# Strassen-like forms made in the attention's output projection, and three more pairs by seven products

## Chip, cores and metric

One core of one Trainium2 chip runs the whole program in one launch. The metric is device time in microseconds (us) of one execution; the result is the median of several. The profile is one execution taken by the hardware profiler. TensorE is called PE, VectorE DVE, ScalarE ACT, GpSimd POOL and SyncE SP, as in the profile.

## The reference

A two-layer trunk on x (512 tokens, width 1024) with a memory of 256 tokens, all in float32. Layer 0 has a hybrid attention mixer, layer 1 an mLSTM mixer; both then have memory cross-attention and a gated convolutional feed-forward network. Cut to what matters:

```python
def conv_ffn(xn, w_up, conv_w, conv_b, w_down):
    h = causal_depthwise_conv(xn @ w_up, conv_w) + conv_b
    g, u = jnp.split(h, 2, axis=-1)
    return (jax.nn.gelu(g) * u) @ w_down

for layer in range(2):
    ...
    x = x + mixed
    x = x + memory_cross_attention(rms_norm(x, xattn_norm[layer]), rms_norm(mem, mem_norm[layer]), ...)
    x = x + conv_ffn(rms_norm(x, ffn_norm[layer]), ffn_w_up[layer], ffn_conv_w[layer],
                     ffn_conv_b[layer], ffn_w_down[layer])
return rms_norm(x, final_norm)
```

The up-projection has 2 x 2816 columns, so 44 blocks of 128. Block p of the gate half and block p of the other half make pair p, with p from 0 to 21. Each pair gives 128 rows of activations for the down-projection.

## The kernel before

Everything is kept transposed: x is eight tiles `x[k]` of 128 features by 512 tokens. A float32 product is made of three matmuls: each operand is split into a high part in the matmul's format and a low remainder (`split`: a copy on ACT, then `sub` on DVE), and `mm3` (L274 to L276) adds high x high, high x low and low x high in PSUM.

**Cross-attention** (`xattn`). `Plan` orders tasks by a time model of PE, ACT and DVE and by priority. Its last stage is `p_out`, the output projection: for each of eight blocks m, 24 matmuls of 512 columns, then `xadd` (L495, x += block) and `xprep` (L469 to L476: the scaled split of x for the next stage, and the sum of squares for its norm).

**Feed-forward** (`ffn_steps`). `Sched` lists tasks for PE, ACT, DVE, SP and POOL, each with a duration, dependencies, a due time as priority, and slots of buffers, and emits them in the order of a simulated run; the framework then orders each engine's instructions from that. `clock` is the sum of PE's durations so far, so `at` is PE's planned time at a pair's start.

- A *plain* pair is two blocks of 8 x `mm3` at 512 columns: 48 matmuls. DVE subtracts the two weights' low parts (1024 columns each) and takes two blocks out of PSUM (L1299).
- A pair by *seven products* treats weights and x as 2 x 2 blocks (the halves of the pair, the halves of the features, the halves of the tokens). Seven products of 12 matmuls at 256 columns replace eight, 84 matmuls in all. Four of them (`p6`, `p5`, `p7`, `p4`) take sums of x's blocks as the moving operand: these *forms* T1 to T4 are made once a layer, in four tiles `th[k]`, `tl[k]` of high and low parts. The weights' sums are made anew for each pair: SP loads half of both blocks into `sa`, POOL's accumulating DMA adds the other block onto it (L1318), DVE makes two more sums (L1340, L1346), and five splits follow. Between products DVE combines blocks (L1380, 256 columns each, through scratch tiles `v`, `u2`, `u3`), and L1401 scales the pair.
- `tail` does the convolution (ACT L1256, four DVE taps L1263), the gelu, the product and the split of the activations `ah`, `al`. For pairs 20 and 21 its due times are 25 us earlier.
- `fill` puts *down* blocks between the products: the down-projection goes by chunks of 4, 4, 4, 4 and 6 pairs, eight blocks each; a block of the first four chunks is 12 matmuls of 512 columns on a weight loaded to `dr`. Chunk c's eight blocks are queued once its pairs are done, at pair 5, 9, 13 and 18; a plain pair takes two, a seven-product pair three. At pair 19 the rest of the queue is cut, and its last four blocks are kept for after pair 21 (`late`). Then the last chunk follows, in layer 1 in `finish`.

Before, `SEVEN` holds pairs 4 to 15 and 17 to 20, 16 of 22. The forms are made by `forms` (L1229 to L1242) during pairs 0 and 1, through the rows `hs` and `sa` as scratch. DVE starts a layer's feed-forward with the last `xprep`, then these forms and the norm's root between pair 0's weights.

Of the kernel before, what the change touches and what calls it, by code (L numbers as in the profile page):

```python
# [9 lines left out]
F32 = mybir.dt.float32  # L10
# [15 lines left out]
SEVEN = (4, 5, 6, 7, 8, 9, 10, 11, 12, 13, 14, 15, 17, 18, 19, 20)  # L26
# [106 lines left out]
class Task:  # L133
    def __init__(self, eng, dur, fn, deps, prio, take, free, lat):
        self.eng, self.dur, self.fn, self.prio, self.lat = eng, dur, fn, prio, lat
        self.deps = [d for d in deps if d is not None]
        self.take, self.free = take, free
        self.end = None


class Sched:
# [8 lines left out]
    def add(self, eng, dur, fn, deps, prio, take=(), free=(), lat=0.25):  # L150
        t = Task(eng, dur, fn, deps, prio, take, free, lat)
        t.n = len(self.tasks)
        self.tasks.append(t)
        return t
# [8 lines left out]
    def run(self):  # L163
# [56 lines left out]
class Builder:  # L220
# [154 lines left out]
    def p_out(self, pl, src, mixed, kdeps, gain, gi, order, prio, reload=False, order0=None):  # L375

        state = {}
        done = []
        for m in range(KB8):
            e = self.p_proj(  # L380
                pl, src[m], mixed, lambda ps, m=m: self.xadd(m, ps, reload), (("D", 0.6),), kdeps=kdeps, order=order, prio=prio + m
            )
            done.append(
                pl.add(lambda m=m: self.xprep(m, gain, gi, state), 0, [e], prio + m, chain=(("A", 0.52), ("D", 0.66), ("A", 0.52)), order=[order0])
            )
        self.state = state
        self.xdone = {k: [d] for k, d in enumerate(done)}
# [337 lines left out]
    def mix0(self):  # L725
        nc, t, tc = self.nc, self.t, self.tc
        with tc.tile_pool(name="mix0", bufs=1, reuse_waits="tile") as mp:
# [61 lines left out]
            def gates(ps):  # L789
                z = rows["z"] = self.til(self.memp, "mem", bufs=8)[:8, :]  # L790
# [135 lines left out]
    def p_memory(self, pl, layer, at, step, order=()):  # L926
# [16 lines left out]
        for k in range(KB8):  # L943

            def prep(k=k):
                both = self.til(mp, "mem", (P, 2, MEM), F32R, bufs=8)
# [46 lines left out]
    def xattn(self, layer):  # L993
        nc, t, tc = self.nc, self.t, self.tc
        with tc.tile_pool(name=f"xa{layer}", bufs=1, reuse_waits="tile") as mp:
            self.mp = mp
            pl = Plan(self.plan, [st["banks"][0] for st in self.fills], s=2, w=2, e=4, q=2, pt=2, wt=3)
            self.pad(mp, 192)
            kth = mp.tile([P, KB8, MEM], F32R, name=f"kth{layer}")
            ktl = mp.tile([P, KB8, MEM], F32R, name=f"ktl{layer}")  # L1000
            self.pad(mp, 64)
            vh = mp.tile([P, 2, DM], F32R, name=f"xvh{layer}")
            vl = mp.tile([P, 2, DM], F32R, name=f"xvl{layer}")
# [4 lines left out]
            for h in range(4):  # L1008
# [49 lines left out]
                def ptget(pts=pts):  # L1058
# [36 lines left out]
                for d in range(2):  # L1095

                    def weigh(h=h, d=d, pts=pts):
# [5 lines left out]
                        mh[b], ml[b] = (self.til(mp, "mixed", dtype=F32R, bufs=8) if h < 2 else self.til(self.memp, "mem", dtype=F32R, bufs=8) for _ in range(2))  # L1103
# [5 lines left out]
            self.p_out(pl, t["xo"][layer], lambda: (mh, ml), kd, "ffn", layer, None, 100)  # L1109
# [8 lines left out]
    def ffn_steps(self, layer, mp):  # L1118
# [23 lines left out]

        def raw_tile(st, tag):
            pool, n, bufs = RAWS[tag]
            st[tag] = self.til(pool, tag, (P, n), bufs=bufs)
            return st[tag]

        def load(st, tag, src, cols, at):
# [4 lines left out]
            return add("SP", 0.0017 * cols, fn, (), at, [(tag, st)], (), 4.0)  # L1153
# [60 lines left out]

        self.pad(mp, 192)
        th, tl = ([mp.tile([P, 1024], F32R, name=f"t{i}{layer}{k}", tag=f"t{i}{k}") for k in range(4)] for i in "hl")
        formed, pads = [], []
# [3 lines left out]

        def forms(k, at):

            st = {}

            def scaled(j):
                if j == 0:
                    st["t"] = hs2[st["_hs"]][:, :, 2:514]
                nc.scalar.activation(st["t"][:, j, :512], self.x[k + 4 * j][:], AF.Identity, scale=self.col("ffn", layer * 8 + k + 4 * j))  # L1229

            def first():
                st["r"] = raw_tile(st, "sa")[:]
                tt_(out=pair(st["r"][:, :512]), in0=pair(st["t"][:, 0, :512]), in1=st["t"][:, :, 256:512], op=ALU.subtract)

            T1, T3, T2, T4 = (slice(256 * i, 256 * i + 256) for i in range(4))
            tt_ = nc.vector.tensor_tensor
            a = add("ACT", ACV, lambda: scaled(0), (), at, [("hs", st)])
            a = add("ACT", ACV, lambda: scaled(1), [a], at)
            a = add("DVE", tt(512), first, [a], at, [("sa", st)])
            a = add("DVE", tt(256), lambda: tt_(out=st["r"][:, T2], in0=st["t"][:, 1, 256:512], in1=st["r"][:, T1], op=ALU.add), [a], at)  # L1240
            a = add("DVE", tt(256), lambda: tt_(out=st["r"][:, T4], in0=st["t"][:, 1, 0:256], in1=st["r"][:, T2], op=ALU.subtract), [a], at, (), [("hs", st)])
            h = add("ACT", act(1024), lambda: nc.scalar.copy(th[k][:], st["r"]), [a], at)  # L1242
            formed.append(add("DVE", tt(1024), lambda: self.sub(tl[k][:], st["r"], th[k][:]), [h], at, (), [("sa", st)]))


        def tail(p, st, deps, at):
# [28 lines left out]
            def hi():  # L1275
                acts[p] = tuple(self.til(mp, n, dtype=F32R, bufs=10) for n in ("ah", "al"))
# [32 lines left out]
        def seven(p, fill):  # L1309
# [11 lines left out]
            b1 = load(sa, "sa", up2[p][:, :, :512], 1024, at - 20.0)  # L1321
# [4 lines left out]
            def small(s, tag):  # L1326
                if tag == "s4" and not pads:
                    pads.append(self.pad(mp, 64))
                s["wh"], s["wl"] = (self.til(mp, tag + i, (P, 512), F32R, bufs=1) for i in "hl")
# [39 lines left out]
            p6 = pe(n, lambda: opened("Y", by, "acc", s2, 0, *T2, "Y", True), [w2, *formed], [("acc", by)], [("s2", s2)])  # L1369
# [13 lines left out]
            tmp = lambda n_: (lambda: st[n_][:])  # L1383
# [27 lines left out]
        def down(c, m, steps=1):  # L1411
# [8 lines left out]
            e = add("DVE", 0.6, lambda: self.xadd(m, d["ps"]), [last, xadded[m], *formed], clock[0] + 3.0, (), [("w", d)])  # L1420
# [218 lines left out]
    def finish(self, mp, ah, al):  # L1639
# [7 lines left out]
        outs = [self.til(mp, f"t{i}{k}", (P, 1024), F32R, bufs=1).bitcast(F32)[:, s] for k in range(4) for i in "hl" for s in (slice(0, 512),)]  # L1647
# [20 lines left out]
        def write(ps, t, f, r, vector):  # L1668
            out = outs.pop(0)
            if vector:  # L1670
                nc.vector.tensor_scalar(out=out[:], in0=ps[:], scalar1=r, scalar2=None, op0=ALU.mult)
            else:
                nc.scalar.activation(out[:], ps[:], AF.Identity, scale=r)
            (nc.sync if f else nc.scalar).dma_start(self.t["y"][t][:, f * 512 : f * 512 + 512], out[:])
# [33 lines left out]
    def run(self):  # L1708
        tc = self.tc
        M = bass.MemoryType.PSUM  # L1710
        with (
# [10 lines left out]
            for layer in range(2):  # L1722
                with tc.tile_pool(name=f"mem{layer}", bufs=1, reuse_waits="tile") as self.memp:
                    (self.mix0, self.mix1)[layer]()
                    self.xattn(layer)
                self.ffn(layer)
# [88 lines left out]
```

## Time and profile before

| what | us |
|---|---|
| median of 3 runs | 1497.57 (1497.55 to 1497.65) |
| profiled execution | 1497.39 |
| its span, first to last instruction | 1495.6 |
| PE busy in the span | 1483.6 |
| DVE busy | 1194.5 |
| ACT busy | 806.0 |
| POOL busy | 57.8 |
| feed-forward of layer 0, on PE | from about 416.7 to 765 |
| feed-forward of layer 1, on PE | from about 1139.6 to 1484 |

The page's first part gives busy time by engine, its second the span in 40 slices of 37.4 us with the busy share in tenths. The stage windows give each engine's busy time between two moments; a number in brackets counts instructions that touch the window. In the instruction rows the first number is the start, the second the duration, then engine, line, operation and tiles. In grouped rows "busy, mean ns" and the idle time before follow the bar.

### The profile page before, as it was taken

How to read it: one execution, taken by the hardware profiler on the slowest of the kernel's cores; microseconds unless marked ns; L12 is line 12 of the kernel's file. 1: busy time of each engine (PE TensorE's matmuls, PEld its weight loads, DVE VectorE, ACT ScalarE, POOL GpSimd, SP SyncE). 2: the span in 40 equal slices, each digit the busy share in tenths (PEclk: the TensorE clock that was granted, in tenths of full speed). 3: DMA queues.
4: the chain of work that ended last, by engine and by line, in shares of the span. 5: the costliest groups of instructions: out<-in, count | busy, mean ns of one | idle time of the engine just before them, and what ended most of it. 6: DMA issues, size and time to landing. Idle time of an engine off the chain costs nothing.

```text
span 1495.6 us, 22361 instructions
## 1 busy us (share of the span) xinstructions
PE 1483.6 (99%) x8426; PEld 1281.9 (86%) x8426; DVE 1194.5 (80%) x2255; ACT 806.0 (54%) x1349; POOL 57.8 (4%) x100
## 2 busy tenths in 40 slices
PE   9999999999999999999999999999999999999998
PEld 7888777888889999999888778888888899998987
DVE  7779795666589999989768857666567999999974
ACT  7777573444466455555446634444444655555544
POOL 0000130000001000000000000000000000000000
PEclk9999999999999999999999999999999999999999
DMA  5212223323237665542232222323323756564322
GB/s 195 85 63 79 85 86 115 125 74 125 85 127 192 168 157 154 148 120 89 75 99 85 71 99 84 99 93 120 113 72 126 183 156 169 149 162 134 94 65 76
DMA packets 60796, 171.76 MB, mean 115 GB/s; under 512 B 6672, under 2 KB 6672, under 8 KB 60688
## 3 DMA queue, kind: packets, MB, share of 16 engines
q1 hardware_dynamic: 55072, 152.43, 31.2%
q0 software_dynamic: 4608, 16.78, 6.6%
q8 instruction: 66, 1.08, 0.3%
q10 hardware_dynamic: 1008, 1.12, 0.2%
q14 instruction: 42, 0.34, 0.1%
HBM read 168.21 MB, written 2.10 MB: 114 GB/s over the span
## 4 chain that ended last, share of the span: by engine, by line
PE 93%; DVE 4%; ACT 2%; issue 1%; DMA 0%; SPq 0%; DVEq 0%; ACTq 0%
PE acc L274 19%; PE acc L276 19%; PE acc L275 19%; PE w L275 5%; PE w L274 5%; PE w L276 5%; PE s L274 3%; PE acc L335 2%; PE s L276 2%; PE acc L337 2%; PE acc L336 2%; PE s L275 2%; PE w L1603 1%; DVE wl L265 1%; PE s L401 1%
## 5 line engine op out<-in xcount | busy, mean ns | idle before, releaser
L274 PE MATMUL acc<-xh,wh 128*128 128x512 f32 (+1 forms) x832 | 301.3, 362 | 0.0
L276 PE MATMUL acc<-xh,wl 128*128 128x512 f32 (+1 forms) x832 | 296.8, 357 | 0.0
L275 PE MATMUL acc<-xl,wh 128*128 128x512 f32 (+1 forms) x832 | 296.6, 356 | 0.0
L265 DVE TENSOR_TENSOR wl<-raw,wh 128x1024 fp32r<-128x1024 f32 (+2 forms) x201 | 240.5, 1197 | 44.2 <-ACT wh L268 39.9
L268 ACT CAST wh<-raw 128x1024 fp32r<-128x1024 f32 (+2 forms) x137 | 140.6, 1029 | 164.7 <-PE acc L275 97.5
L275 PEld LDWEIGHTS acc<-xl,wh 128*128 128x128 f32 x832 | 157.2, 189 | 22.0
L276 PEld LDWEIGHTS acc<-xh,wl 128*128 128x128 f32 x832 | 156.2, 188 | 22.7
L274 PEld LDWEIGHTS acc<-xh,wh 128*128 128x128 f32 x832 | 156.3, 188 | 22.1
L1263 DVE SCALAR_TENSOR_TENSOR c<-hs,vec,c 128x512 f32<-128x512 f32 x176 | 128.8, 746 | 4.5 <-ACT c L1256 3.7
L275 PE MATMUL w<-al,wh 128*128 128x512 f32 x304 | 118.6, 390 | 0.0
L274 PE MATMUL w<-ah,wh 128*128 128x512 f32 x304 | 118.5, 390 | 0.0
L276 PE MATMUL w<-ah,wl 128*128 128x512 f32 x304 | 118.4, 389 | 0.0
L1256 ACT ACTIVATE c<-hs,vec 128x512 f32<-128x512 f32 x88 | 69.8, 813 | 52.9 <-DVE hs L1401 46.5
L276 PEld LDWEIGHTS w<-ah,wl 128*128 128x128 f32 x304 | 57.0, 188 | 12.0
L274 PEld LDWEIGHTS w<-ah,wh 128*128 128x128 f32 x304 | 57.1, 188 | 10.2
L275 PEld LDWEIGHTS w<-al,wh 128*128 128x128 f32 x304 | 57.1, 188 | 10.1
L495 DVE TENSOR_TENSOR x<-w,x 128x512 f32<-128x512 f32 x72 | 49.3, 685 | 16.1 <-PE w L276 16.1
L274 PE MATMUL acc<-mem,wh 128*128 128x256 f32 (+1 forms) x192 | 61.5, 320 | 0.0
L276 PE MATMUL acc<-mem,wl 128*128 128x256 f32 (+1 forms) x192 | 61.0, 318 | 0.0
L275 PE MATMUL acc<-mem,wh 128*128 128x256 f32 (+1 forms) x192 | 60.8, 317 | 0.0
L495 DVE TENSOR_TENSOR x<-acc,x 128x512 f32<-128x512 f32 x32 | 22.1, 690 | 46.6 <-PE acc L276 46.6
L1165 ACT CAST wh<-dr 128x512 fp32r<-128x512 f32 x64 | 39.5, 617 | 35.7 <-PE w L275 18.4
(373 smaller groups left out, 3798.2 us busy)
## 6 DMA issues: line engine op xcount, KB each, us to landing
raw<-in_up_dram SPq DMA_DIRECT2D x56, 512.0 KB, 3.3
dr<-in_down_dram SPq DMA_DIRECT2D x64, 256.0 KB, 2.9
sa<-in_up_dram SPq DMA_DIRECT2D x32, 512.0 KB, 3.5
sa<-in_up_dram POOLq DMA_DIRECT2D x32, 512.0 KB, 5.6
raw<-in_xk_dram SPq DMA_DIRECT2D x16, 512.0 KB, 3.2
raw<-in_wo_dram SPq DMA_DIRECT2D x16, 512.0 KB, 3.3
raw<-in_xq_dram SPq DMA_DIRECT2D x16, 512.0 KB, 3.2
raw<-in_xv_dram SPq DMA_DIRECT2D x16, 512.0 KB, 3.2
```

What stands on the lines that cost most here:

```text
L265: self.nc.vector.tensor_tensor(out=lo, in0=v, in1=hi.bitcast(F32), op=ALU.subtract)
L268: self.nc.scalar.copy(hi, v)
L274: mm(out, wh, xh, start=first, stop=False, skip_group_check=parts)
L275: mm(out, wh, xl, start=False, stop=False, skip_group_check=parts)
L276: mm(out, wl, xh, start=False, stop=last, skip_group_check=parts)
L335: mm(ps, xh[k][:, ts], wh[:, ws], start=(k == 0), stop=False)
L336: mm(ps, xh[k][:, ts], wl[:, ws], start=False, stop=False)
L337: mm(ps, xl[k][:, ts], wh[:, ws], start=False, stop=(k == 7))
L495: self.nc.vector.tensor_tensor(out=self.x[m][:], in0=ps[:], in1=self.x[m][:], op=ALU.add)
L1165: nc.scalar.copy(st["wh"][:, :cols], st[tag][:, :cols])
L1256: nc.scalar.activation(st["c_"][:, j, :], hs()[:, j, 2:514], AF.Identity, scale=self.col("cw", (layer * 3 + 2) * 44 + blk), bias=self.col( ...
L1263: nc.vector.scalar_tensor_tensor(out=c, in0=hs()[:, j, n : n + 512], scalar=w, in1=c, op0=ALU.mult, op1=ALU.add)
```

## The change

Pairs 3, 16 and 21 go by seven products too, so pairs 3 to 21 without a gap. `forms` is taken out of the feed-forward. `p_forms`, a task of the attention's plan, makes the same forms with the same operations; `p_out` of the cross-attention visits its blocks in the order 0, 4, 1, 5, 2, 6, 3, 7, so that form k follows as soon as x[k] and x[k + 4] are done. Two empty planner tasks stand for this work at the start of the feed-forward's plan. A task can have an earliest time (`after`), and the loads of the weight sums of pairs 3, 4 and 5 have one, 16 us ahead of the pair. The late list keeps six blocks in place of four; five are in the queue by then.

To hold the forms from one stage to the next, tiles move: a pool `kv` of four tiles holds the attention's keys and values and then the forms; the memory's tiles stay open as `mem0` to `mem7` and serve, in turn, the memory, half of the attention's outputs, and in the feed-forward `s2`, `a22`, `ra`, `dr` and one `sb`; `v` lies in the memory's norm tile, `u2` and `u3` in the scratch `sqt` of two buffers. `finish` writes its output through the `kv` tiles.

```diff
-SEVEN = (4, 5, 6, 7, 8, 9, 10, 11, 12, 13, 14, 15, 17, 18, 19, 20)
+SEVEN = (3, 4, 5, 6, 7, 8, 9, 10, 11, 12, 13, 14, 15, 16, 17, 18, 19, 20, 21)
...
-                    at = 0.0 if e == "-" else now[e]
+                    at = t.after if e == "-" else max(now[e], t.after)
...
-    def p_out(self, pl, src, mixed, kdeps, gain, gi, order, prio, reload=False, order0=None):
+    def p_out(self, pl, src, mixed, kdeps, gain, gi, order, prio, reload=False, order0=None, ms=range(KB8), after=None):
...
+            if after and m >= 4:
+                after(m - 4, done[m] + done[m - 4], prio + n)
...
+    def p_forms(self, pl, layer, k, deps, prio):
...
+        th, tl = self.form(0, k), self.form(1, k)
+        def one():
+            g = st["g"] = self.til(self.mp, "pth", (P, 2, 512), F32)
+            r = st["r"] = self.til(self.mp, "ptl", (P, 2, 512), F32)[:].rearrange("p a b -> p (a b)")
+            for j in range(2):
+                nc.scalar.activation(g[:, j, :], self.x[k + 4 * j][:], AF.Identity, scale=self.col("ffn", layer * 8 + k + 4 * j))
+            tt(out=r[:, :512].rearrange("p (a b) -> p a b", a=2), in0=g[:, 0, :].rearrange("p (a b) -> p a b", a=2), in1=g[:, :, 256:512], op=ALU.subtract)
+            tt(out=r[:, T2], in0=g[:, 1, 256:512], in1=r[:, T1], op=ALU.add)
+            tt(out=r[:, T4], in0=g[:, 1, 0:256], in1=r[:, T2], op=ALU.subtract)
+        def two():
+            nc.scalar.copy(th, st["r"])
+            self.sub(tl, st["r"], th)
+        a = pl.add(one, 0, deps, prio, chain=(("A", 1.04), ("D", 1.28)))
+        pl.add(two, 0, [a], prio, chain=(("A", 0.95), ("D", 1.14)))
...
-            self.p_out(pl, t["xo"][layer], lambda: (mh, ml), kd, "ffn", layer, None, 100)
+            self.p_out(pl, t["xo"][layer], lambda: (mh, ml), kd, "ffn", layer, None, 100, ms=(0, 4, 1, 5, 2, 6, 3, 7), after=lambda *a: self.p_forms(pl, layer, *a))
...
+        HOMES = {}
+        for n, (tag, i) in enumerate([("s2h", 0), ("s2l", 0), ("a22h", 0), ("a22l", 0), ("ra", 0), ("dr", 0), ("dr", 1), ("sb", 1)]):
+            HOMES[tag, i] = f"mem{n}"
...
+        add("DVE", 4.0, None, (), -20.0)
+        add("ACT", 3.0, None, (), -20.0)
...
-            b1 = load(sa, "sa", up2[p][:, :, :512], 1024, at - 20.0)
+            b1 = load(sa, "sa", up2[p][:, :, :512], 1024, at - 20.0, at - 16 if p < 6 else 0.0)
...
-            p6 = pe(n, lambda: opened("Y", by, "acc", s2, 0, *T2, "Y", True), [w2, *formed], [("acc", by)], [("s2", s2)])
+            p6 = pe(n, lambda: opened("Y", by, "acc", s2, 0, *T2, "Y", True), [w2], [("acc", by)], [("s2", s2)])
...
-                st["v_"] = self.til(mp, "v", (P, 256), bufs=1)
+                st["v_"] = self.til(self.memp, f"memrb", (P, 256), bufs=1)
...
-                    st[tag] = self.til(mp, tag, (P, 256), bufs=1)
+                    st[tag] = self.til(self.sp, "sqt")[:, :256]
...
-                queue, late = queue[:-4], queue[-4:]
+                queue, late = queue[:-6], queue[-6:]
             (seven if p in SEVEN else plain)(p, fill if p >= 5 else lambda: None)
-            if p < 2:
-                for k in (2 * p, 2 * p + 1):
-                    forms(k, clock[0] + 4.0 * (k % 2))
...
-                self.ffn(layer)
+                    with tc.tile_pool(name=f"kv{layer}", bufs=1, reuse_waits="tile") as self.kvp:
+                        self.pad(self.kvp, 192)
+                        self.kv = [self.til(self.kvp, f"kv{i}", (P, 2048), F32R, bufs=1) for i in range(4)]
+                        self.xattn(layer)
+                        self.ffn(layer)
```

More of the change, by code (lines that the diff above doesn't have):

```diff
@@ L133, with __init__ @@
 class Task:
-    def __init__(self, eng, dur, fn, deps, prio, take, free, lat):
-        self.eng, self.dur, self.fn, self.prio, self.lat = eng, dur, fn, prio, lat
+    def __init__(self, eng, dur, fn, deps, prio, take, free, lat, after):
+        self.eng, self.dur, self.fn, self.prio, self.lat, self.after = eng, dur, fn, prio, lat, after
         self.deps = [d for d in deps if d is not None]
@@ L148, in __init__, with add @@
         self.turn = {r: 0 for r in res}
-    def add(self, eng, dur, fn, deps, prio, take=(), free=(), lat=0.25):
-        t = Task(eng, dur, fn, deps, prio, take, free, lat)
+    def add(self, eng, dur, fn, deps, prio, take=(), free=(), lat=0.25, after=0.0):
+        t = Task(eng, dur, fn, deps, prio, take, free, lat, after)
         t.n = len(self.tasks)
@@ L373, in xs @@
         return self.xh, self.xl
-    def p_out(self, pl, src, mixed, kdeps, gain, gi, order, prio, reload=False, order0=None):
+    def p_out(self, pl, src, mixed, kdeps, gain, gi, order, prio, reload=False, order0=None, ms=range(KB8), after=None):
         state = {}
-        done = []
-        for m in range(KB8):
+        done = {}
+        for n, m in enumerate(ms):
             e = self.p_proj(
-                pl, src[m], mixed, lambda ps, m=m: self.xadd(m, ps, reload), (("D", 0.6),), kdeps=kdeps, order=order, prio=prio + m
+                pl, src[m], mixed, lambda ps, m=m: self.xadd(m, ps, reload), (("D", 0.6),), kdeps=kdeps, order=order, prio=prio + n
@@ L382, in p_out @@
             )
-            done.append(
-                pl.add(lambda m=m: self.xprep(m, gain, gi, state), 0, [e], prio + m, chain=(("A", 0.52), ("D", 0.66), ("A", 0.52)), order=[order0])
-            )
+            done[m] = [pl.add(lambda m=m: self.xprep(m, gain, gi, state), 0, [e], prio + n, chain=(("A", 0.52), ("D", 0.66), ("A", 0.52)), order=[order0])]
+            if after and m >= 4:
+                after(m - 4, done[m] + done[m - 4], prio + n)
         self.state = state
-        self.xdone = {k: [d] for k, d in enumerate(done)}
+        self.xdone = done
@@ new lines, in p_forms @@
+    def p_forms(self, pl, layer, k, deps, prio):
+        nc = self.nc
+        tt = nc.vector.tensor_tensor
+        T1, T3, T2, T4 = (slice(256 * i, 256 * i + 256) for i in range(4))
+        th, tl = self.form(0, k), self.form(1, k)
+        st = {}
+        def one():
[11 more added lines that the diff above has]
+        pl.add(two, 0, [a], prio, chain=(("A", 0.95), ("D", 1.14)))
@@ L389, in evac_tok, with form @@
+    def form(self, i, k):
+        return self.kv[2 * i + k // 2][:, k % 2 * 1024 : k % 2 * 1024 + 1024]
     def evac_tok(self, ps, r, hi, lo):
@@ L1102, in weigh @@
                         b = 2 * h + d
-                        mh[b], ml[b] = (self.til(mp, "mixed", dtype=F32R, bufs=8) if h < 2 else self.til(self.memp, "mem", dtype=F32R, bufs=8) for _ in range(2))
+                        if b == 0:
+                            self.pad(mp, 64)
+                        mh[b], ml[b] = (
+                            self.til(mp, "mixed", dtype=F32R, bufs=8) if h < 2 else self.til(self.memp, f"mem{2 * b - 8 + i}", dtype=F32R, bufs=1) for i in range(2)
+                        )
                         self.split(mh[b][:], ml[b][:], ps[:])
@@ L1212, in norm @@
             return add("ACT", 0.52, None, [c], c.prio)
+        th, tl = ([self.form(i, k) for k in range(4)] for i in range(2))
+        pads = []
         self.pad(mp, 192)
-        th, tl = ([mp.tile([P, 1024], F32R, name=f"t{i}{layer}{k}", tag=f"t{i}{k}") for k in range(4)] for i in "hl")
-        formed, pads = [], []
         hs2 = [mp.tile([P, 2, 514], F32, name=f"hs{layer}{i}") for i in range(2)]
@@ L1220, in ffn_steps @@
             nc.gpsimd.memset(h[:, :, 0:2], 0.0)
[L1222 to L1243, printed above, removed]
+        add("DVE", 4.0, None, (), -20.0)
+        add("ACT", 3.0, None, (), -20.0)
         def tail(p, st, deps, at):
@@ L1419, in down @@
                     joined([last], last.prio, [("act", acted[first + k].st)])
-            e = add("DVE", 0.6, lambda: self.xadd(m, d["ps"]), [last, xadded[m], *formed], clock[0] + 3.0, (), [("w", d)])
+            e = add("DVE", 0.6, lambda: self.xadd(m, d["ps"]), [last, xadded[m]], clock[0] + 3.0, (), [("w", d)])
             xadded[m] = e
@@ L1646, in finish @@
         HALF = [slice(0, 256), slice(256, 512)]
-        outs = [self.til(mp, f"t{i}{k}", (P, 1024), F32R, bufs=1).bitcast(F32)[:, s] for k in range(4) for i in "hl" for s in (slice(0, 512),)]
+        outs = [kv[:, 512 * i : 512 * i + 512] for kv in (self.til(self.kvp, f"kv{i}", (P, 2048), bufs=1) for i in range(2)) for i in range(4)]
         def add(m, ps, c):
```

38 lines of the change are left out of this document (22 added, 16 removed).

## The prediction

> **What bounds the kernel now.** I read the page first, then TensorE's waits, then stages of the feed-forward network (the stage windows), and last VectorE's instructions in order of time.
>
> ```profile
> span 1495.6 us, 22361 instructions
> PE 1483.6 (99%) x8426; PEld 1281.9 (86%) x8426; DVE 1194.5 (80%) x2255; ACT 806.0 (54%) x1349; POOL 57.8 (4%) x100
> DVE  7779795666589999989768857666567999999974
> ...
> PE s L436 <- DVE sqt L430: 1.8, 5, 0.7
> PE acc L514 <- DVE ones L506: 1.1, 1, 1.1
> ```
>
> TensorE (PE) is busy for 99% of the span, and its longest sum of waits on one cause is 1.8 us. So time falls only where matmul time falls, and only as long as the others keep up. The row of VectorE (DVE) names the one that may not: most of its nines lie in the two feed-forward stages, where the change acts. The profiled execution took 1497.39 us, 1.8 more than its span; the median is 1497.57, and I carry differences over to it.
>
> ```profile
> core 0: us, PE busy (x) PEld busy (x) DVE busy (x) ACT busy (x) POOL busy (x), PEclk, DMA share, GB/s
> 645.42:656.30 10.88, 10.88 (x49) 9.01 (x48) 9.84 (x14) 5.62 (x8) 0.00 (x0) 1.00 0.29 97
> 584.20:596.73 12.53, 12.53 (x110) 12.53 (x108) 11.99 (x20) 7.60 (x12) 0.86 (x1) 1.00 0.64 166
> 496.73:499.46 2.73, 2.73 (x14) 2.25 (x13) 2.73 (x6) 1.24 (x2) 0.00 (x0) 1.00 0.69 134
> 606.38:609.55 3.17, 3.08 (x25) 2.87 (x24) 3.13 (x6) 1.67 (x2) 0.00 (x0) 1.00 0.67 226
> 1329.15:1332.17 3.02, 3.02 (x25) 2.85 (x24) 3.02 (x6) 1.67 (x2) 0.00 (x0) 1.00 0.61 197
> 405.80:416.68 10.88, 10.88 (x50) 9.01 (x49) 6.36 (x8) 4.40 (x6) 0.00 (x0) 1.00 0.34 104
> 428.85:461.98 33.13, 33.13 (x147) 27.40 (x146) 31.04 (x45) 23.26 (x31) 1.86 (x2) 1.00 0.51 144
> 477.38:512.00 34.62, 34.62 (x230) 31.68 (x229) 34.51 (x56) 19.83 (x31) 0.86 (x2) 1.00 0.56 146
> 645.42:717.78 72.36, 72.32 (x481) 66.24 (x480) 65.47 (x99) 37.49 (x57) 0.87 (x1) 1.00 0.31 87
> ```
>
> The first row is plain pair 16 of layer 0: 48 matmuls of 512 columns (a count takes in the neighbour at the edge). The second holds nine products of 12 matmuls of 256 columns (108 weight loads). The third is one down block. In the eighth DVE works 34.51 of 34.62 us, and PE still loses nothing: DVE can be full without holding PE.
>
> **Term 1: the products.** A plain pair costs PE 10.88 us. A pair by seven products costs 7 x 12.53 / 9 = 9.75. That is 1.13 less a pair. Pairs 3, 16 and 21 change in both layers: 6 x 1.13 = 6.80 us off PE. The granted clock is 1.00 in all these rows, so no clock enters.
>
> The Trainium skill ("TensorE: Matmul & The Clock Gate", section "Back-to-back issue gap") gives an isolated spacing of N/2.4 + 2.5 ns, 109 ns at 256 columns and 216 at 512; by it, as an estimate, the six pairs would give 6 x (48 x 0.2158 - 84 x 0.1092) = 7.1 us. The rows show 116 and 227 ns, so the measured 6.80 is used.
>
> **Term 2: the forms.** A form is, on ACT, two scalings of 512 and a copy of 1024; on DVE three small sums and a subtraction over 1024. How long DVE takes from one start to the next, when it is full, stands here:
>
> ```profile
> 464.84 0.68 DVE L1340 TENSOR_TENSOR sb<-sa,raw 128x512 f32<-128x512 f32 x1
> 465.45 0.68 DVE L265 TENSOR_TENSOR s4l<-sb,s4h 128x512 fp32r<-128x512 f32 x1
> 466.05 1.22 DVE L265 TENSOR_TENSOR wl<-raw,wh 128x1024 fp32r<-128x1024 f32 x1
> 467.18 0.42 DVE L1380 TENSOR_TENSOR u<-acc,v 128x256 f32<-128x256 f32 x1
> 467.52 0.74 DVE L1263 SCALAR_TENSOR_TENSOR c<-hs,vec,c 128x512 f32<-128x512 f32 x1
> 468.18 0.69 DVE L265 TENSOR_TENSOR s2l<-sb,s2h 128x512 fp32r<-128x512 f32 x1
> ```
>
> By these starts a subtraction or sum over 512 takes 0.605 us, over 1024 1.13, over 256 0.34, a convolution tap 0.66. A form is then 0.605 + 2 x 0.34 + 1.13 = 2.42 us of DVE, four a layer 9.7. ACT's part comes from these two groups: 2 x 0.71 + 1.04 = 2.5.
>
> ```profile
> L1229 ACT ACTIVATE hs<-x,vec 128x512 f32<-128x512 f32 x8 | 5.5, 713 | 0.0
> L1242 ACT CAST th<-sa 128x1024 fp32r<-128x1024 f32 x4 | 4.2, 1042 | 1.9 <-DVE sa L1241 1.9
> ...
> 419.74 0.68 DVE L470 TENSOR_TENSOR sq<-sq,sqt 128x512 f32<-128x512 f32 x1
> 420.34 0.69 DVE L1233 TENSOR_TENSOR sa<-hs 128x512 f32<-128x512 f32 x1
> ```
>
> In their new place two output blocks take PE 10.88 us (window 405.80:416.68) beside 6.36 of DVE and 4.40 of ACT. One form more makes 8.8 and 6.9, still below 10.88: cost 0. Without that cover it would be up to 2.4 us a form. Only the fourth has no output block after it. But in before the first form already starts at 420.34, right behind the last square sum at 419.74, so the fourth takes a place that was taken, and the norm's chain behind it is no later: 0, bounded by one form, 2.4 us, if PE stood for it. The forms issue no DMA. The new order of the blocks changes no count.
>
> The feed-forward start loses 9.7 us of DVE work and gains a seven-product pair. Such a pair takes DVE 7 x 0.605 + 3 x 1.13 + 5 x 0.34 + 4 x 0.66 = 11.97 us; a plain pair takes 4 x 0.605 + 2 x 1.13 + 4 x 0.66 = 7.32. The difference is 4.65, so about 5 us of DVE come free while PE loses 1.13. In window 428.85:461.98 DVE had 31.04 of 33.13. I expect no stall from DVE there.
>
> **Term 3: pairs 16 to 21, where DVE gets tight.** No down blocks are queued in pairs 16 and 17, three in pair 18; the longer late list takes the one of pair 19. In before, window 645.42:717.78 has DVE at 65.47 of 72.36. The change adds 4.65 for pair 16, and for pair 21 the part before its products end: 11.97 less its tail and the last two steps (0.34 + 1.13 + 4 x 0.66 + 2 x 0.605 = 5.3) against 2.87 for the plain one (two weight subtractions, one evacuation): 3.8. It takes away one down block's 2 x 0.605 = 1.2. DVE: 72.7 us. PE: 72.36 - 2 x 1.13 - 2.73 = 67.4. By that DVE is 5.3 us short. This is the upper bound, since the busy time counts instructions that stood alone at their full duration, 0.08 above the spacing of a full DVE; were all 99 such, 7.9 us would be recovered and nothing be short. So the shortage lies in -2.6 to 5.3 us a layer.
>
> What covers it: the five late blocks, 5 x 2.73 = 13.65 us of PE for 6 us of DVE. They need no result of pairs 16 to 21, so the planner can pull one forward where a product waits. Then only the end counts: pair 21's activation must be ready for the last chunk.
>
> ```profile
> 725.72 0.69 DVE L265 TENSOR_TENSOR al<-c,ah 128x512 fp32r<-128x512 f32 x1
> ```
>
> In before it ends at 726.41, 8.63 after PE left the pairs at 717.78, and four late blocks (10.9) cover it. After: 8.63 + 0.34 + 1.22 - 0.69 = 9.5, plus a backlog of up to 5.3: 14.8 at most. Five blocks give 13.65, and the last activation is read only by the sixth step of the next block, 5 x 0.68 = 3.4 later: 17.05. Covered; if blocks are pulled forward, both sides shrink alike.
>
> What remains is small: a product that finds its operand late. Before shows the size behind pairs without down blocks: 24 small matmuls took 3.17 and 3.02 (windows 606.38 and 1329.15), where 24 x 12.53 / 108 = 2.78 is normal: 0.39 and 0.24. After has four such places more a layer (pairs 3, 16, 19, 21). I take 0.25 each, 1.0 a layer, 2.0 in all, near these rows; the bounds are -0.3 a layer (the present losses vanish too) and 5.3.
>
> **Term 4: loads and shared buffers.** One answer, 0. The early rows of the load queue:
>
> ```profile
> 414.06 0.38 SPq L1151 DMA_DIRECT2D ra<-in_up_dram  x1
> 414.50 0.90 SPq L1151 DMA_DIRECT2D dr<-in_down_dram  x2
> 419.08 0.33 SPq L1151 DMA_DIRECT2D raw<-in_up_dram  x1
> ...
> sa<-in_up_dram SPq DMA_DIRECT2D x8, 512.0 KB, 4.2
> sa<-in_up_dram POOLq DMA_DIRECT2D x7, 512.0 KB, 5.8
> ```
>
> `ra` and `dr` now lie where the attention's outputs lie, which the last output block reads until 416.68; behind them on SP stands the raw load that went out only at 419.08. The later sums of pairs 3 to 5 (SP load, then POOL's accumulating load) need 4.2 + 5.8 + casts and subtraction of 1.04 + 1.22 = 12.3 us; the first is issued 16 us ahead of its pair and used by the third product, 2.8 after the pair's start. Margin: 6.5 us. The sharing of `v`, `u2`, `u3` with other scratch keeps the same number of buffers.
>
> **Sum.** -6.80 + 2.0 = -4.8 us: 1492.6 for a profiled execution, 1492.8 for the median.
>
> **Rivals.** *Full gain:* DVE never holds PE. For it: window 477.38:512.00, DVE full, PE unhurt. Against: the 0.39 and 0.24. Time 1490.8, at best 1490.2.
>
> *The sums of pairs 3 to 5 come late:* three seven-product pairs in a row now stand at the start, each wanting 1.75 MB (two halves of 512 KB for the sum, 512 raw, 256 for the last block). Window 584.20:596.73 moved 166 GB/s at a DMA share of 0.64, so there is room. Every us beyond the margin of 6.5 costs 1 a layer; three pairs late by 0.8 eat 4.8 of the two layers: about 1497.6, no change.
>
> *VectorE bounds pairs 19 to 21 (slower).* These three have no down block at all: PE wants 29.2 us, DVE 3 x 11.97 = 35.9. If the late blocks aren't pulled forward (their own weights need DVE and a weight buffer behind those of pair 21, and the tails of pairs 20 and 21 are ordered 25 us early, ahead of pair 21's operands), PE stands for the 5.3 us: 2 x 5.3 - 6.80 = +3.8, 1501.4. It decides at 3 x 1.13 = 3.4 us of stall a layer. For it: the eights and nines of DVE; against: the 13.65 us of ready PE work. The Trainium skill ("VectorE: DVE Perf Modes", section "The DRAIN you can't avoid") says that the next operation does not start until the pipe is empty, which speaks for full durations and so for this rival; the rows disagree: the 0.42 us instruction of 467.18 would end at 467.60, the next starts at 467.52.
>
> *The change doesn't do what it says:* the forms slip behind the output projection. Then DVE has 9.7 us back at the start, and its window there is as full as before; I count this with the late sums.
>
> **How the numbers follow.** Forecast (stall of 0.4 to 1.8 a layer) 0.54; full gain 0.12; late sums 0.14; VectorE bound 0.20. About 0.2%, 3 us, is what a measurement tells from no change. Faster: forecast and full gain, 0.66. Within 0.2%: late sums and the mildest part of the last, 0.18. Slower: 0.16. The range runs from 1490.2 (no stall left) up into the VectorE rival, 1499.0; about 0.03 below and 0.15 above are left out. The likeliest case alone: 1490.8 + 2 x 0.4 to 2 x 1.8, so 1491.6 to 1494.4.
>
> **What would show it.** The profile after should have 128 x 256 matmuls in place of the 512-column ones of pairs 3, 16, 21 (108 to 9 products in 12.5 us still), forms between the output blocks, DVE near full from pair 16 on, and late blocks inside pairs 20 or 21. PE gaps in pairs 19 to 21 above 3.4 us a layer, or a first gap at pair 3 that ends with a DMA, would make the forecast wrong.

## The result, and the profile after

The changed kernel takes 1502.56 us (median of 7 runs, 1501.21 to 1504.08); the kernel before, beside it, 1497.65 (1497.12 to 1498.57). The ratio is 1.0032, 95% interval 1.0022 to 1.0041: slower by 4.9 us, where 4.8 us faster were forecast. The profiled execution took 1501.64 us, 4.25 more than that of before; its span is 4.0 longer.

The page's first part and its row of VectorE, then the first rows of TensorE's waits (us in total, times, longest):

```profile
span 1499.6 us, 22932 instructions
PE 1481.0 (99%) x8642; PEld 1287.1 (86%) x8642; DVE 1219.3 (81%) x2309; ACT 821.0 (55%) x1379; POOL 63.8 (4%) x106
DVE  7779795766789999999868857666668899999984
```

```profile
PE acc L274 <- ACT memrb L1399: 3.8, 2, 2.2
PE s L464 <- DVE sqt L458: 1.8, 5, 0.7
PE s L274 <- DVE hs L1404: 1.7, 2, 1.4
```

TensorE's busy time fell by 2.6 us, so the products did get cheaper. (The fall is less than term 1's 6.8 in part because products at the reduced clock, shown below, count as busy.) Two waits are new, 3.8 and 1.7 us, each twice: once a layer, and each time at pair 3. `memrb` at L1399 is the copy of -X which a seven-product pair makes between its first product and the next one on the same bank.

The stage windows say how much each layer lost. The bounds are the first matmul of the norm's sums ahead of the feed-forward and the corresponding norm behind it (in layer 1 the last such sums). The first two rows are before's. The other five are the changed kernel's: its two layers, then three stretches around pair 3.

```profile
420.48:767.73 347.25, 347.12 (x2184) 312.95 (x2183) 316.68 (x496) 187.23 (x280) 14.38 (x18) 1.00 0.49 134
1143.40:1486.86 343.46, 343.24 (x2231) 312.81 (x2230) 308.87 (x498) 187.14 (x285) 13.70 (x16) 1.00 0.47 128
```

```profile
420.80:769.02 348.22, 344.74 (x2291) 314.71 (x2291) 321.85 (x511) 188.34 (x286) 17.00 (x21) 1.00 0.53 141
1144.77:1490.79 346.02, 342.85 (x2338) 316.53 (x2338) 314.61 (x513) 188.26 (x291) 16.29 (x19) 1.00 0.51 134
...
455.00:465.00 10.00, 6.79 (x56) 6.20 (x54) 9.62 (x15) 5.60 (x9) 0.86 (x1) 1.00 0.56 130
1178.00:1182.60 4.60, 2.41 (x21) 2.21 (x20) 4.00 (x6) 3.62 (x6) 0.87 (x1) 1.00 0.33 114
1182.64:1186.05 3.41, 3.41 (x19) 3.41 (x18) 3.33 (x6) 1.24 (x2) 0.00 (x0) 0.50 0.88 149
```

Layer 0's stage is 0.97 us longer, layer 1's 2.56. In the first stretch around pair 3 (layer 0) TensorE stands for 3.2 of 10 us, in the second (layer 1) for 2.2 of 4.6. The third adds a cost that no wait shows: behind that gap the granted clock is 0.50 for 3.41 us, and half of that, 1.7 us, is lost. In layer 0 the clock stays at 1.00. Together that is 7.1 us.

Why is the copy late? The first product of pair 3 in layer 0, then, well ahead of it, SP's and POOL's queues and VectorE's instructions in order of time:

```profile
451.37 0.28 PE L274 MATMUL acc<-xh,wh 128*128 128x256 f32 x1
```

```profile
423.92 0.43 SPq L1194 DMA_DIRECT2D sa<-in_up_dram  x1
426.81 0.94 SPq L1194 DMA_DIRECT2D sa<-in_up_dram  x2
...
428.36 1.01 POOL L1342 DMA_DIRECT2D sa<-in_up_dram  x1 [54.01 <-DMA sa<-in_up_dram]
432.35 0.86 POOL L1342 DMA_DIRECT2D sa<-in_up_dram  x1 [2.98 <-ACT c L1278]
```

```profile
434.30 0.75 DVE L1285 SCALAR_TENSOR_TENSOR c<-hs,vec,c 128x512 f32<-128x512 f32 x1
436.66 0.69 DVE L1364 TENSOR_TENSOR sb<-sa,raw 128x512 f32<-128x512 f32 x1 [1.61 <-DMA sa<-in_up_dram]
437.27 0.68 DVE L1323 TENSOR_TENSOR hs<-acc,rb 128x512 f32<-128x512 f32 x1
440.23 0.69 DVE L1364 TENSOR_TENSOR mem<-sa,raw 128x512 f32<-128x512 f32 x1 [2.28 <-DMA sa<-in_up_dram]
440.84 0.68 DVE L1295 TENSOR_TENSOR c<-c 128x512 f32<-128x512 f32 x1
```

The first weight sums of pairs 3 and 4 (L1364) stand at the head of VectorE's queue 15 and 11 us ahead of pair 3, and wait 1.61 and 2.28 us for the accumulating loads; in layer 1 the same two wait 2.18 and 2.30. Behind them stand a plain pair's evacuation (L1323) and a tail (L1295) whose inputs are there: that block's last matmul started at 434.83, and the tail's gelu ended at 435.06. VectorE takes neither ahead of the waiting sum. ScalarE's convolutions and casts wait for these in turn (3.55 us at 441.56 for L1295's result). The lag is still there at pair 3, in ScalarE's rows and then in TensorE's:

```profile
455.58 0.63 ACT L1293 ACTIVATE c<-c 128x512 f32<-128x512 f32 x1 [0.67 <-DVE c L1285]
456.18 0.81 ACT L1278 ACTIVATE c<-hs,vec 128x512 f32<-128x512 f32 x1
456.90 0.36 ACT L1399 ACTIVATE memrb<-acc 128x256 f32<-128x256 f32 x1
```

```profile
457.32 0.39 PE L274 MATMUL acc<-xh,wh 128*128 128x256 f32 x1 [1.63 <-ACT memrb L1399]
```

The copy that TensorE stands for comes third, behind a gelu that waited for VectorE; the product that it reads had its last matmul at 452.67. That is the theory for the runs (A): **VectorE stands at two sums that were put into its queue too early; the lag reaches TensorE at pair 3.** It is read from the order of waits here; the runs below test it. Before, the forms used `sa`'s three buffers in turn, and the sums' loads came after them:

```profile
444.11 5.42 SPq L1151 DMA_DIRECT2D sa<-in_up_dram  x2
```

```profile
458.77 0.68 DVE L1340 TENSOR_TENSOR sb<-sa,raw 128x512 f32<-128x512 f32 x1
```

They left at 444.11, and their first sum (pair 4's) waited for nothing. The sums' loads, now of pairs 3, 4 and 5, leave at 423.92 to 427.75. How crowded that makes the transfers shows in two windows, the first two rows of before, the last two of after:

```profile
428.85:435.00 6.15, 6.15 (x28) 5.07 (x27) 5.09 (x8) 5.13 (x7) 0.00 (x0) 1.00 0.25 89
435.00:441.00 6.00, 6.00 (x28) 4.97 (x27) 4.97 (x8) 4.68 (x7) 0.00 (x0) 1.00 0.14 33
```

```profile
428.85:435.00 6.15, 6.15 (x29) 5.10 (x28) 5.02 (x7) 4.82 (x6) 2.23 (x3) 1.00 0.96 284
435.00:441.00 6.00, 6.00 (x28) 4.95 (x28) 2.11 (x5) 1.73 (x3) 0.00 (x0) 1.00 1.06 255
```

The DMA share is about 1 where it was 0.25 and 0.14, and VectorE's busy time in the second window falls from 4.97 to 2.11. So a rival (B) is that the loads are at fault: too many at once, or issued at the wrong time, whatever VectorE's order.

### The profile page after: what moved, and what is told of

It is laid out like the page before. It is cut to its first block, busy times and chain, and to the rows that moved or that the text cites. A ratio compares the mean times of both kernels' runs of the same rounds, so it can differ in the third digit from the quotient of the medians.

```text
span 1499.6 us, 22932 instructions
## 1 busy us (share of the span) xinstructions
PE 1481.0 (99%) x8642; PEld 1287.1 (86%) x8642; DVE 1219.3 (81%) x2309; ACT 821.0 (55%) x1379; POOL 63.8 (4%) x106
## 4 chain that ended last, share of the span: by engine, by line
PE 85%; DVE 9%; ACT 2%; issue 2%; DMA 2%; SPq 0%; DVEq 0%; ACTq 0%
PE acc L274 16%; PE acc L276 16%; PE acc L275 16%; PE w L276 5%; PE w L274 5%; PE w L275 5%; PE s L274 3%; PE s L276 3%; PE s L275 3%; PE acc L335 2%; PE acc L337 2%; PE acc L336 2%; DVE wl L265 2%; DVE c L1285 1%; PE w L1624 1%
## 5 line engine op out<-in xcount | busy, mean ns | idle before, releaser
L274 PE MATMUL acc<-xh,wh 128*128 128x512 f32 (+1 forms) x784 | 277.8, 355 | 3.8 <-ACT memrb L1399 3.8
L276 PE MATMUL acc<-xh,wl 128*128 128x512 f32 (+1 forms) x784 | 273.2, 349 | 0.0
L275 PE MATMUL acc<-xl,wh 128*128 128x512 f32 (+1 forms) x784 | 272.8, 348 | 0.0
L265 DVE TENSOR_TENSOR wl<-raw,wh 128x1024 fp32r<-128x1024 f32 (+2 forms) x195 | 232.9, 1195 | 42.3 <-ACT wh L268 39.5
L274 PEld LDWEIGHTS acc<-xh,wh 128*128 128x128 f32 x784 | 147.5, 188 | 22.8 <-ACT memrb L1399 4.2
L275 PEld LDWEIGHTS acc<-xl,wh 128*128 128x128 f32 x784 | 148.5, 189 | 18.5
L276 PEld LDWEIGHTS acc<-xh,wl 128*128 128x128 f32 x784 | 147.5, 188 | 19.1
L274 PE MATMUL acc<-kv,mem 128*128 128x256 f32 x304 | 84.6, 279 | 0.0
L275 PE MATMUL acc<-kv,mem 128*128 128x256 f32 x304 | 84.4, 278 | 0.0
L276 PE MATMUL acc<-kv,mem 128*128 128x256 f32 x304 | 84.3, 277 | 0.0
L1208 ACT CAST wh<-mem 128x512 fp32r<-128x512 f32 x64 | 39.6, 618 | 43.8 <-PE acc L275 18.0
L274 PE MATMUL acc<-mem,wh 128*128 128x256 f32 (+1 forms) x192 | 61.5, 320 | 0.0
```

Of the source, the lines that this page charges most:

```text
L265: self.nc.vector.tensor_tensor(out=lo, in0=v, in1=hi.bitcast(F32), op=ALU.subtract)
L274: mm(out, wh, xh, start=first, stop=False, skip_group_check=parts)
L275: mm(out, wh, xl, start=False, stop=False, skip_group_check=parts)
L276: mm(out, wl, xh, start=False, stop=last, skip_group_check=parts)
L1208: nc.scalar.copy(st["wh"][:, :cols], st[tag][:, :cols])
```

## The experiments

A helper, `behind(engine, on)`, puts an instruction in an engine's queue behind the last one that the planner emitted for that engine. Without it the final order of a queue may differ from the planner's, and here it does.

**VectorE held.** The sums' loads stay where they are.

```diff
-                tt_(out=raw_tile(sb, "sb")[:], in0=sa["sa"][:, 512:], in1=r2["raw"][:, :512], op=ALU.add)
+                to = raw_tile(sb, "sb")[:]
+                with self.behind(nc.vector.engine, p < 6):
+                    tt_(out=to, in0=sa["sa"][:, 512:], in1=r2["raw"][:, :512], op=ALU.add)
```

> The changed kernel, but on VectorE the first weight sum of pairs 3, 4 and 5 (L1364) is queued behind the VectorE instruction that the planner emitted just before it, so the framework cannot put it ahead. Theory A (VectorE stands at the head of its queue for the landing of those sums' accumulating loads, 1.6 + 2.3 us a layer, and this lag reaches TensorE in pair 3): no such wait on VectorE, the TensorE gaps at pair 3 (3.7 us in layer 0, 2.8 us in layer 1 with 1.6 us of half clock behind) vanish, 1493 to 1495 us. Rival B (pairs 3 to 5 by seven products without down blocks are too much for VectorE and ScalarE in any order): gaps stay, 1500 to 1503. Rival C (the DMA engines are full and the operands land too late in any order): the gaps stay and end with a DMA, 1499 to 1503.

Measured: 1495.44 us, ratio to before 0.9983 (0.9974 to 0.9993). One edit of order turns 4.9 us slower into 2.5 faster. The two sums in VectorE's order of time, and the two layers' windows:

```profile
443.73 0.68 DVE L1373 TENSOR_TENSOR sb<-sa,raw 128x512 f32<-128x512 f32 x1
453.55 0.68 DVE L1373 TENSOR_TENSOR mem<-sa,raw 128x512 f32<-128x512 f32 x1
```

```profile
420.74:765.76 345.02, 344.48 (x2292) 314.38 (x2291) 321.24 (x511) 187.92 (x286) 16.99 (x21) 1.00 0.53 142
1141.63:1483.73 342.10, 341.22 (x2338) 314.66 (x2338) 313.71 (x513) 187.73 (x291) 16.29 (x19) 1.00 0.51 136
```

They run 7 and 13 us later than in the changed kernel, and no wait stands at them. The loads left SP at 423.86 and 426.75, as in the changed kernel, and the crowd of transfers is still there, as the same two windows show:

```profile
428.85:435.00 6.15, 6.15 (x28) 5.07 (x27) 5.07 (x7) 4.87 (x6) 2.21 (x3) 1.00 0.99 263
435.00:441.00 6.00, 6.00 (x28) 4.96 (x27) 4.11 (x6) 3.06 (x4) 0.00 (x0) 1.00 1.07 255
```

It cost nothing there: B falls as far as the crowd goes.

**The sums' loads held on SP.** VectorE's order is left free.

```diff
-                nc.sync.dma_start(to.rearrange("p (a b) -> p a b", a=2) if len(src.shape) == 3 else to, src)
+                with self.behind(nc.sync.engine, after > 0.0):
+                    nc.sync.dma_start(to.rearrange("p (a b) -> p a b", a=2) if len(src.shape) == 3 else to, src)
```

> The changed kernel, but on SyncE the loads of the sums of pairs 3, 4 and 5 are queued behind the load that the planner emitted just before them, so they go out later, one by one. Theory A: the bunch of loads at the start (DMA share 0.96 to 1.06 for 12 us) is spread, VectorE waits less than 1 us a layer for a sum, 1493 to 1496. Rival B: gaps at pair 3 stay, 1500 to 1503. Rival C: as theory A or, if the later loads are too late for pair 3, a gap there that ends with a DMA, 1498 or more.

Measured: 1509.48 us, ratio 1.0077 (1.0062 to 1.0092), a clear miss: it was expected to help. TensorE's first wait, VectorE's sums grouped for 428 to 470 us, and the window of the reduced clock:

```profile
PE acc L281 <- ACT memrb L1407: 9.2, 2, 5.0
```

```profile
L1372 DVE TENSOR_TENSOR sb<-sa,raw 128x512 f32<-128x512 f32 x2 | 1.4, 691 | 5.3 <-DMA sa<-in_up_dram 5.3
L1372 DVE TENSOR_TENSOR mem<-sa,raw 128x512 f32<-128x512 f32 x1 | 0.7, 693 | 3.5 <-DMA sa<-in_up_dram 3.5
```

```profile
458.30:465.13 6.83, 4.25 (x20) 4.25 (x21) 5.82 (x9) 3.59 (x7) 0.48 (x1) 0.50 0.59 97
```

The sums still come early in VectorE's queue, and their data now come later: the waits grow from 3.9 to 8.8 us in layer 0, TensorE's longest wait from 2.2 to 5.0, and the granted clock is 0.50 for 6.83 us. What counts is the distance between place in the queue and landing, not the time of the load.

**No later plan.** The planner's `after` is taken out.

```diff
-            b1 = load(sa, "sa", up2[p][:, :, :512], 1024, at - 20.0, at - 16 if p < 6 else 0.0)
+            b1 = load(sa, "sa", up2[p][:, :, :512], 1024, at - 20.0)
```

> The changed kernel without the later plan: the loads of the sums of pairs 3 to 5 are planned as before, 20 us ahead of their pairs. Their order on SP against the other loads stays as in the changed kernel, and on VectorE the first weight sums of pairs 3 and 4 stand at the same two places of the queue. Theory A (the loss is VectorE standing at weight sums that wait for the accumulating loads, because the order of the queue puts them early; the later plan does next to nothing): as slow as the changed kernel, 1500 to 1504 us, VectorE's waits for DMA of sa 3 to 4.5 us a layer. Theory B (the later plan makes the loads land late): the wait goes, 1494 to 1497.

Measured: 1503.03 us, ratio 1.0037 (1.0022 to 1.0052), as the changed kernel. Layer 0's row:

```profile
L1364 DVE TENSOR_TENSOR mem<-sa,raw 128x512 f32<-128x512 f32 x2 | 1.4, 686 | 4.2 <-DMA raw<-in_up_dram 4.2
```

VectorE waits 4.2 us in layer 0, all of it at pair 4's sum, and now for that sum's other operand. The plain halves (`raw`) leave SP at nearly the same time, but in 420 to 445 us they took 5.9 us to land (median) against 4.0 in the changed kernel; that the three loads let go ahead of them push them back is my reading and not tested. The part of the change that should have spread the loads makes no difference that can be seen; A holds.

**Both holds.** The two edits above together.

> Both holds: VectorE's first weight sums of pairs 3 to 5 queued where the plan has them, and the sums' loads queued on SP where the plan has them (first 3, second 16, third 21 us later than in the changed kernel). The data of the three sums are then there at about 440, 456 and 460; with VectorE held they are wanted at 443.7, 453.6 and 463.9. Theory A: one wait of some 2.5 us at pair 4's sum in each layer, little of it on TensorE, 1495 to 1499, far below the 1509.5 of the SP hold alone. Rival (late loads hurt by themselves, through PE waiting for weights or through DMA load at another place, whatever VectorE's order): 1503 to 1510.

Measured: 1495.00 us, ratio 0.9984 (0.9975 to 0.9994). The first weight sums of layer 0:

```profile
L1374 DVE TENSOR_TENSOR mem<-sa,raw 128x512 f32<-128x512 f32 x2 | 1.4, 684 | 0.0
L1374 DVE TENSOR_TENSOR sb<-sa,raw 128x512 f32<-128x512 f32 x2 | 1.4, 682 | 0.0
```

Later loads like those that stood beside 1509.48 cost nothing once VectorE's sums stand later in its queue. Even the 2.5 us that I expected at pair 4's sum don't appear; its load left at 437.54 here, not at 442.93 as with SP's hold alone, so this run was a milder trial of late loads than I had reckoned.

**Pair 3 plain, and the move alone.** Two kernels without holds: pair 3 taken out of `SEVEN`, and `SEVEN` as before, so that the forms and tiles move (the later plan and the late list stay as changed).

```diff
-SEVEN = (3, 4, 5, 6, 7, 8, 9, 10, 11, 12, 13, 14, 15, 16, 17, 18, 19, 20, 21)
+SEVEN = (4, 5, 6, 7, 8, 9, 10, 11, 12, 13, 14, 15, 16, 17, 18, 19, 20, 21)
```

```diff
-SEVEN = (3, 4, 5, 6, 7, 8, 9, 10, 11, 12, 13, 14, 15, 16, 17, 18, 19, 20, 21)
+SEVEN = (4, 5, 6, 7, 8, 9, 10, 11, 12, 13, 14, 15, 17, 18, 19, 20)
```

> The changed kernel with pair 3 plain again (pairs 4 to 21 by seven products). Theory A: the gaps at pair 3 go, four conversions of 1.13 us stay, pairs 16 to 21 cost up to 1 us a layer: 1493 to 1495. Rival B: the gaps move to pair 4 at about half their size, 1496 to 1499. If instead pairs 16 and 21 were what costs, the time stays above 1498.

> The changed kernel with the pairs of before by seven products (4 to 15, 17 to 20): forms in the output projection, buffers moved, sums of the early pairs planned later, five late blocks. Theory A: all of this is hidden, 1497.0 to 1498.2, as before. If the move of the forms or of the buffers costs by itself: 1499 or more.

Measured: 1494.96 us without pair 3 (ratio 0.9980, 0.9971 to 0.9989) and 1498.55 for the move alone (1.0006, 0.9997 to 1.0016). The loss needs pair 3, and the move by itself brings no measurable cost or gain. SP's loads and VectorE's first sum of the move alone in layer 0:

```profile
423.49 0.43 SPq L1194 DMA_DIRECT2D sa<-in_up_dram  x1
426.43 0.90 SPq L1194 DMA_DIRECT2D sa<-in_up_dram  x2
```

```profile
444.37 0.69 DVE L1364 TENSOR_TENSOR sb<-sa,raw 128x512 f32<-128x512 f32 x1 [0.96 <-DMA raw<-in_up_dram]
```

With the pairs of before and the forms gone from the feed-forward, the loads leave at 423.49 and 426.43 instead of 444.11: the move alone sets them free. The first sum, pair 4's, comes at 444.37 and waits 0.96 us; it is pair 3 that puts two sums at 436.66 and 440.23, where they wait 3.9.

**Pair 3 plain, with VectorE held.**

> VectorE's hold, and pair 3 plain (4 to 21 at seven products). If pair 3 with the hold is worth its 1.13 us a layer less the 0.25 us of TensorE gaps left there: 1.8 us slower than the hold alone, 1496.5 to 1498. Rival (pair 3 costs TensorE as much as it saves even with the hold, since VectorE has no room there): 1494 to 1495.5, as the run without pair 3 and without a hold.

Measured: 1496.04 us, ratio 0.9987 (0.9977 to 0.9997). That is 0.6 us above VectorE's hold alone, which the intervals of the two ratios don't tell apart, 1.0 above both holds, and 1.1 above the 1494.96 of the same pairs without a hold. What pair 3 is worth with the hold stays open between nothing and its full 2.26 us.

**Pairs 16 and 21 plain, with VectorE held.**

```diff
-SEVEN = (3, 4, 5, 6, 7, 8, 9, 10, 11, 12, 13, 14, 15, 16, 17, 18, 19, 20, 21)
+SEVEN = (3, 4, 5, 6, 7, 8, 9, 10, 11, 12, 13, 14, 15, 17, 18, 19, 20)
```

> VectorE's hold as in the run before, and pairs 16 and 21 plain again (pair 3 stays at seven products). Sizes the end stage. By the prediction's terms: two pairs a layer lose 1.13 us each of TensorE's gain (+4.5 in all) and give back a stall of about 1.0 us a layer (-2.0): 2.5 us slower than the hold alone, 1497 to 1499. Rival (VectorE bounds pairs 16 to 21 so that these two bring nothing): the same as or faster than the hold alone, 1494 to 1495.5.

Measured: 1497.87 us, ratio 0.9999 (0.9990 to 1.0009), 2.4 slower than the hold alone against 2.5 expected. So the two pairs together bring about what the terms say, and the rival by which VectorE eats their gain falls. The layers' windows agree, with 346.61 and 343.64 us against the 345.02 and 342.10 shown above, 3.1 in all:

```profile
421.05:767.66 346.61, 346.39 (x2220) 313.57 (x2220) 313.98 (x493) 182.87 (x276) 15.30 (x19) 1.00 0.50 137
1143.46:1487.10 343.64, 343.14 (x2266) 313.72 (x2266) 306.43 (x495) 182.66 (x281) 14.56 (x17) 1.00 0.48 131
```

**Late blocks.** Both holds, with six, four and eight blocks kept for the end.

```diff
-                queue, late = queue[:-6], queue[-6:]
+                queue, late = queue[:-4], queue[-4:]
```

> The kernel with both holds once more, as the measure for the two beside it and for a closer comparison with the kernel before. Theory A: 1494.5 to 1496, faster than before by more than 0.1%. Rival (its lead was the spread of runs): within 0.1% of before.

> Both holds, and four blocks instead of six are kept back for the end of the feed-forward. If the stall of pairs 16 to 21 is VectorE's shortage, covered by late blocks (Term 3), two blocks fewer (5.4 us of TensorE work) leave more of it bare: up to 1 us a layer slower than the run beside it, 1495 to 1497. Rival (the number of late blocks doesn't set that stall): within 0.5 us of it.

> Both holds, and eight blocks instead of six are kept back. If Term 3's shortage is what is left at the end: up to 0.8 us a layer faster than the run with six, 1493 to 1495, with the gaps at pairs 18 to 21 gone. Rival (the gaps there come from the order in which blocks and pairs are pulled forward, not from too few blocks): within 0.5 us of the run with six, with gaps of the same size at other places.

Measured: six 1495.20 us (ratio 0.9980, 0.9971 to 0.9989), four 1493.74 (0.9973, 0.9963 to 0.9983), eight 1495.31 (0.9982, 0.9974 to 0.9991). I expected fewer late blocks to cost and more to help; fewer did not hurt. Eight is no trial at all: only five blocks are in the queue at pair 19, so six and eight both keep all five back, and the two traces hold the same instructions in the same order on every engine. The 1495.31 repeats the 1495.20, and whether more than five would help was not run. The windows of six, then of four:

```profile
420.50:765.83 345.33, 344.75 (x2292) 314.50 (x2291) 321.33 (x511) 187.80 (x286) 17.05 (x21) 1.00 0.53 142
1141.84:1484.21 342.37, 341.26 (x2339) 314.62 (x2338) 313.83 (x513) 187.91 (x291) 16.32 (x19) 1.00 0.51 136
```

```profile
420.47:765.31 344.84, 344.19 (x2292) 314.68 (x2292) 321.37 (x511) 187.71 (x286) 17.05 (x21) 1.00 0.53 142
1141.26:1482.96 341.70, 340.90 (x2338) 314.88 (x2338) 313.90 (x513) 187.74 (x291) 16.32 (x19) 1.00 0.52 136
```

With four, the stages are 0.5 and 0.7 us shorter. The intervals of the two ratios overlap, so a gain over five is likely and not settled. The kernel with both holds and four late blocks is the fastest of all: 4.2 us below before, 8.8 below the changed kernel.

## Why the prediction was wrong

**Term 1 held.** Two neighbouring pairs of the changed kernel, 14 products without a down block:

```profile
652.41:671.87 19.46, 19.46 (x171) 19.46 (x170) 19.38 (x32) 10.85 (x18) 1.70 (x2) 1.00 0.69 178
```

That is 9.73 us a pair where 9.75 stood in the sum.

**Term 2 held nearly where it spoke of the output projection** (the norm's sums start at 420.80 against 420.48, and with VectorE held all that lies outside the two feed-forward stages is 0.5 us longer, where 0 was taken), **and failed in its last sentence**, "I expect no stall from DVE there". I counted VectorE's work and found 5 us free. What was taken away had also spaced the queue: without the forms the sums' loads leave 20 us earlier (the move alone shows it), and pair 3's sum moves up with them. VectorE stood idle at a queue's head while it had work.

**Term 3 was right in kind and too small.** With the stall at pair 3 gone, the two layers with VectorE held gain 347.25 - 345.02 = 2.23 and 343.46 - 342.10 = 1.36 us, against 3 x 1.13 - 1.0 = 2.4. The stall left is then 1.2 and 2.0 a layer where 1.0 was taken; with four late blocks the gains are 2.41 and 1.76, so 1.0 and 1.6. The cover by late blocks was rightly seen as enough; four were no worse than five. But the stall is not at two of the four places that the term named. With VectorE held, the 204 small matmuls from pair 16 to the start of pair 18 (layer 0, 645.10 to 668.71) took 23.61 us and the 216 from pair 19 into pair 21 (682.98 to 708.16) 25.18, 116 and 117 ns each as in term 1, and layer 1 gives the same within 0.04 us: no delay of 0.25 at pairs 16 and 19. By the starts of the matmuls, an estimate, some 0.8 us a layer more than before lie around pairs 3 and 4 instead, and about 1 us at the stage's end. That the size came as near as it did was in part luck.

**Term 4 was the step that failed**: its "One answer, 0" for loads and shared buffers. It gave the sums "16 us ahead of its pair", taken from the planned time, and a margin of 6.5 us before lateness. SP in fact sends them at 423.92 to 427.75, 24 to 27 us ahead of pair 3, earlier than the planner's order had them (with both held, 426.21, 437.54 and 446.94). The data were there at 436.66 and 440.23, the later of them eleven us ahead of pair 3's start at 451.37, so no pair's data were late. The harm lay at another place than the margin measured: at the instruction that stands at the head of VectorE's queue until the data come. In place of 0 the runs show 7.1 us: 1502.56 - 1495.44, with nothing changed but the place of those sums in the queue (7.4 by each kernel's ratio to before), and 3.2 + 2.2 + 1.7 us in the stretches around pair 3.

**The rivals.** *The sums of pairs 3 to 5 come late* named the right loads, but had the wrong mechanism and price: 4.8 us for three pairs late by 0.8, where VectorE stood 3.9 and 4.5 us at its queue's head and a gap was followed by a halved clock, 7.1 us in all. The check I gave, "a first gap at pair 3 that ends with a DMA", had the place right and the end wrong: TensorE's gap ends with ScalarE's copy, and the DMA is what VectorE waited for 15 us earlier. *VectorE bounds pairs 19 to 21* came out near in time (1501.4) by luck, and wrong in cause: in the changed kernel too the 216 small matmuls of pairs 19 to 21 (686.13 to 711.33) took 25.20 us, 117 ns each, and the gaps are at pair 3. *Full gain* did not occur.

Without the step that failed the sum -4.8 would still have been too good. For the change as planned, with the queues held, the chip gives -2.5 (VectorE's alone) and -3.1 and -2.8 (both). In the profile with VectorE held, whose span is 3.1 us shorter, the terms add up: -6.8 for the products, 3.2 of stall where 2.0 was taken, and 0.5 outside the feed-forward. The -4.2 of four late blocks is nearer to the forecast, but that is another kernel.

## What to carry to other kernels

When a change removes work that held buffers, ask what may start earlier without it: loads, and the instructions that wait for them, may move up in the queues, whatever times a planner gave them. Read an engine's queue for an instruction that waits on a transfer while ready work stands behind it; here a later load made that worse, and a later place in the queue mended it. A count of an engine's work says nothing about its order.

## What the runs showed of the hardware that was not expected

A TensorE gap can cost more than its length. A wait of 2.2 us (the changed kernel, layer 1) was followed by a granted clock of 0.50 for 3.41 us. With the loads held on SP, a wait of 4.2 us (layer 1) was followed by 3.41 us again, and one of 5.0 (layer 0) came with 6.83 us, which began inside the gap; the changed kernel's 1.6 us wait of layer 0 left the clock at 1.00. The Trainium skill ("TensorE: Matmul & The Clock Gate", section "HAM oscillation — how this bites in real kernels") warns of idle gaps above about 3.4 us. The reduced stretches fit that length once and twice, but here a wait of 2.2 us was already enough.
